# Values products of two attentions: split fp32r operands on the full array, or fp32 operands on two 64-column halves

## The chip, the cores and the metric

One core of a Trainium2 chip runs the whole kernel. The metric is device time in microseconds (us), the median of several executions. Beside it stands one profiled execution, whose trace gives the rows below.

## What is computed

Two layers of a hybrid decoder on x of 512 tokens by 1024 columns, all in float32. Each layer has a forgetting attention ("fox", 8 heads of 64) and a native sparse attention ("nsa", 8 heads of 64, two key/value heads; here a selected, a sliding-window and a compressed branch), then an MLP. What matters here is the last line of each attention, for one head and a block of 128 queries:

```python
p = softmax(q @ k.T * scale + bias, masked)     # 128 x 512 at most, causal
o = p @ v                                       # v: 512 x 64
# nsa: o_n = g0 * o_cmp + g1 * o_sel + g2 * o_win, then o_n @ w_o_nsa
```

## The kernel before

TensorE multiplies in two ways here. In fp32r, one pass over the moving columns, an operand is split into a high part and the remainder ("h", "lo"), and a product is made of two or three matmuls that accumulate in PSUM. In fp32, with operands unsplit, each matmul of the program becomes two recorded instructions (a weight load and a matmul each). Transposes on TensorE are fp32 with the identity.

`layer` (L781) first projects the values of all heads by token (`token_proj`). It splits them into `VF` (fox, L802 to L809) and `VN` (nsa, L811 to L824): 64 columns of high part and 64 columns of remainder side by side for each head, so that one 128-column weight load holds both. ScalarE (ACT) writes the high part, VectorE (DVE) the remainder. `forget` (L713) is a chain of small DVE steps that ends in a matmul (L738).

`attend` (L507) runs the units of an attention. A unit is one head of fox, or one head of one nsa branch; there are 8 units in fox and 16 in nsa in each layer, 48 in all. In step t it interleaves three generators and a filler: `scores` of unit t (two matmuls for each of four query blocks, then the DVE's masked minimum at L417 and ACT's exponential at L418, and at the end the scaling by the reciprocal sums, L449 and L451), `transposes` of unit t-1 (ten 128x128 transposes in three PSUM banks, L464; ACT writes the high part `pth`, L468, DVE the remainder `ptl`, L469), and `values` of unit t-2. In every round each generator advances once, and then the filler, which is the projections of the layer (`gemm`, L209, 512-column matmuls, six for a step), advances by `FOX_FILL` = 1.8 or `NSA_FILL` = 0.95 steps. The program's instructions get priorities in this order of issue; a scheduler then puts each engine's instructions in a fixed order when the kernel is built, an instruction being placed by priority among those that are ready.

`values` (L473) makes eight matmuls for a unit: key blocks 0 to 3 against 512, 384, 256 and 128 query columns, each with `pth` and `ptl`, stationary 128 columns (v high | v remainder). The two halves of the output bank O (partitions 0 to 63 and 64 to 127) have then to be added: `out_half` (L491) copies one half on ACT (L496) and adds on DVE (L497) into the pair's tile, once for each head; `out_pair` (L499) splits the finished pair of heads for the next projection. In nsa the two branches of a head accumulate in one bank, and `after` (L891) adds the compressed branch with one 512-column fp32r matmul on `self.vz` (L892).

`compress` (L538) already has a block of 64-column fp32 products (`product`, L573 to L584): two products with different operands go to partitions 0 to 63 and 64 to 127 of one bank, in turn; the first has its normal priority and the others are put 60 places ahead, so that they follow it at once. There are eight products in a block and four blocks in a layer (L575).

Of the kernel before, what the change touches and what calls it, by code (L numbers as in the profile page):

```python
# [11 lines left out]
F32 = mybir.dt.float32  # L12
F32R = mybir.dt.float32r
AF = mybir.ActivationFunctionType
OP = mybir.AluOpType
# [4 lines left out]
T = 512  # L20
KT = D // 128
NB = T // 128
# [120 lines left out]
class Body:  # L143
# [309 lines left out]
    def transposes(self, u):  # L453
        nc = self.nc
        E = u["E"]
        u["pt"] = []
        for g in range(3):
            ps = self.p("PT")
            if g < 2:
                todo = [(i, g) for i in range(g, NB)]  # L460
            else:
                todo = [(3, 3), (2, 2), (3, 2)]
            for j, (i, b) in enumerate(todo):
                nc.tensor.transpose(ps[:, j * 128:(j + 1) * 128], E[i][:, b * 128:(b + 1) * 128], self.ident)  # L464
            n = 128 * len(todo)
            h = self.t("t2", [128, T], F32R, name="pth")
            lo = self.t("t2", [128, T], F32R, name="ptl")
            nc.scalar.copy(h[:, :n], ps[:, :n])  # L468
            nc.vector.tensor_sub(lo[:, :n], ps[:, :n], h[:, :n].bitcast(F32))  # L469
            u["pt"].append((h, lo))  # L470
            yield

    def values(self, u):  # L473
        nc = self.nc
        if u.get("first", True):
            u["O"][0] = self.p("O")
        O = u["O"][0]
        first = u.get("first", True)
        pt = u["pt"]
        last = u.get("last", True)  # L480
        todo = [(0, 0, 0, 512), (1, 1, 0, 384), (2, 2, 128, 256), (3, 2, 0, 128)]
        for b, g, o, n in todo:
            v = u["v"](b)
            for f in range(2):
                nc.tensor.matmul(O[:, T - n:], v, pt[g][f][:, o:o + n],  # L485
                                 start=first and b == 0 and f == 0, stop=last and b == 3 and f == 1)
            yield
        if "after" in u:
            u["after"]()

    def out_half(self, O, o, e):  # L491

        nc = self.nc
        t = self.t("tmp", [128, T])
        s, f = slice(64 * e, 64 * e + 64), slice(64 * (1 - e), 64 * (1 - e) + 64)
        nc.scalar.copy(t[s], O[f])  # L496
        nc.vector.tensor_add(o[s], O[s], t[s])  # L497

    def out_pair(self, o):  # L499
        nc = self.nc  # L500
# [6 lines left out]
    def attend(self, units, fill, rate, lead):  # L507


        n = len(units)  # L510
        owed = 0.0
        for _ in range(lead):
            next(fill)
        for t in range(n + 2):
            gens = []
            if t < n:
                while not units[t]["ready"]():
                    next(fill)
                gens.append(self.scores(units[t]))
            if 1 <= t <= n:  # L520
                gens.append(self.transposes(units[t - 1]))
            if t >= 2:
                gens.append(self.values(units[t - 2]))
            while gens:
                for g in list(gens):
                    try:
                        next(g)
                    except StopIteration:
                        gens.remove(g)
                owed += rate  # L530
# [7 lines left out]
    def compress(self, kc, vc, small, l):  # L538

        nc, a = self.nc, self.a  # L540
        A = []
        for x, pos in ((kc, "pos_k"), (vc, "pos_v")):
            t = [self.t("t2", [128, 8, 2, 32], name="ca") for _ in range(2)]
            v = x.rearrange("p (n j r) -> p r j n", j=8, r=2)
            for half in range(2):
                nc.vector.memset(t[half][:, :, 1, 31], 0.0)
                o = OFF[pos] + 8 * half
# [39 lines left out]
        h = self.t("tmp", [128, 256])  # L587
        nc.scalar.copy(h, hp[:, :256])
        pt = self.p("S")
# [4 lines left out]
        g = self.t("tmp", [128, 4, 64], name="g")  # L594
# [25 lines left out]
        k = self.t("tmp", [128, 64])  # L620
# [8 lines left out]
        for e in range(2):  # L629
            s, c = slice(64 * e, 64 * e + 64), slice(64 + 32 * e, 96 + 32 * e)  # L630
            nc.scalar.copy(self.kcz[s, :, 0, c], k2[s])
            nc.gpsimd.tensor_sub(self.kcz[s, :, 1, c], k2[s], self.kcz[s, :, 0, c].bitcast(F32))
        v = self.t("tmp", [128, 2, 64])
# [2 lines left out]
            nc.vector.scalar_tensor_tensor(v[:, hk], pv[:, hk * 64:hk * 64 + 64], 0.5, b2v, op0=OP.mult, op1=OP.add)  # L636
        for k in range(4):
            s = slice(32 * k, 32 * k + 32)
            z = self.vz[s, :, k % 2]
            nc.scalar.copy(z[:, :, :64], v[s])  # L640
            nc.gpsimd.tensor_sub(z[:, :, 64:], v[s], z[:, :, :64].bitcast(F32))

    def cmp_probs(self, hk):

# [136 lines left out]
    def layer(self, l, u):  # L781
        nc, a = self.nc, self.a
# [18 lines left out]
                            self.CHUNKS[l])  # L801
        VF = []  # L802
        for b in range(NB):
            v = self.t("va", [128, 8, 128], F32R, name="vf")
            pv = va[b].rearrange("p (h d) -> p h d", h=8)
            nc.scalar.activation(v[:, :, :64], pv, AF.Copy, scale=rc[:, b:b + 1])
            nc.vector.scalar_tensor_tensor(v[:, :, 64:], pv, rc[:, b:b + 1], v[:, :, :64].bitcast(F32),
                                           op0=OP.mult, op1=OP.subtract)
            VF.append(v)  # L809
        run(g)  # L810
        VN = self.t("vn", [128, NB, 4, 128], F32R)  # L811
        z = self.t("z", [128, NB, 8])
        th = self.t("th", [128, NB, 24])
        rch = self.t("s4", [128, NB], name="rch")
        nc.vector.tensor_scalar(rch, rc, 0.5, None, op0=OP.mult)
        for b in range(NB):
            pv = g2[b][:, :256].rearrange("p (h d) -> p h d", h=4)
# [4 lines left out]
            nc.scalar.activation(VN[:, b, :, :64], pv, AF.Copy, scale=r)  # L822
            nc.vector.scalar_tensor_tensor(VN[:, b, :, 64:], pv, r, VN[:, b, :, :64].bitcast(F32),
                                           op0=OP.mult, op1=OP.subtract)  # L824
# [10 lines left out]
        st = {}  # L835
# [7 lines left out]
        def fox_unit(h):  # L843
            p, e = divmod(h, 2)
            un = dict(q=lambda: st["qa", p][0][:, e], qx=lambda: st["qa", p][1][e], k=lambda: st["ka", p][:, e], O=[None],
                      ready=lambda: ("qa", p) in st and ("ka", p) in st,
                      v=lambda b: VF[b][:, h])

            def after():
                if e == 0:  # L850
                    st["oa", p] = self.t("tmp2", [128, T], name="o")
                self.out_half(un["O"][0], st["oa", p], e)
                if e == 1:
                    st["oa", p] = self.out_pair(st["oa", p])
            un["after"] = after
            return un

# [28 lines left out]
        def nsa_units(h):  # L886
            p, e = divmod(h, 2)
            hk, r = divmod(h, 4)
            O = [None]

            def after():  # L891
                nc.tensor.matmul(O[0], self.vz[:, hk, r % 2], self.pc[hk][r // 2], start=False, stop=True)  # L892
                if e == 0:
                    st["ob", p] = self.t("tmp2", [128, T], name="o")
                self.out_half(O[0], st["ob", p], e)
                if e == 1:
                    st["ob", p] = self.out_pair(st["ob", p])
            q = lambda: st["qb", p][:, e]
            b_ = dict(ready=lambda: hk in self.pc, q=q, k=lambda: st["kw"][:, hk], O=O,
                      v=lambda b: VN[:, b, 2 + hk], first=False, last=False, gate=lambda: gt[:, :, 2, h], after=after)  # L900
            a_ = dict(ready=lambda: ("qb", p) in st and "kw" in st, q=q, k=lambda: st["ks"][:, hk], O=O,
                      v=lambda b: VN[:, b, hk], last=False, gate=lambda: gt[:, :, 1, h], mate=b_,
                      kk=lambda: self.kk[:, :, hk].rearrange("p f b t -> p f (b t)"))
            return [a_, b_]
# [32 lines left out]

        units = []
        for h in range(0, 8, 2):
            (a0, b0), (a1, b1) = nsa_units(h), nsa_units(h + 1)  # L940
# [180 lines left out]
class Pairs:  # L1121
# [275 lines left out]
    def product(self, ps, k, i, xs, new):  # L1397

        h, lo = self.ops[k][i]
        n = len(xs[i])  # L1400

        def mm(w, x, **kw):
            self.nc.tensor.matmul(ps, w, x, skip_group_check=True, **kw)  # L1403

        for p in range(n):
            c = slice(p * 128, (p + 1) * 128)
            xh, xl = xs[i][p]
            mm(h[:, c], xh, start=new and p == 0, stop=False)
            mm(h[:, c], xl, start=False, stop=False)
            mm(lo[:, c], xh, start=False, stop=p == n - 1)  # L1410
# [403 lines left out]
```

## Time and profile before

| | us |
|---|---|
| time before, median of 3 runs | 1467.99 (1467.97 to 1468.05) |
| profiled execution, first to last instruction | 1466.7 |
| difference, outside the profiled span | 1.3 |
| TensorE matmul (PE) busy | 1451.1, 99% |
| TensorE weight load (PEld) busy | 1262.2, 86% |
| DVE busy | 1207.9, 82% |
| ACT busy | 917.8, 63% |
| mean granted TensorE clock | 0.997 |

A matmul's recorded duration includes the way through the array, so the durations of neighbours overlap and a busy PE says little. What a matmul costs its engine is read from the start of one to the start of the next: a 512-column gemm matmul lasts 0.39 us and the next one starts 0.23 us later. Layer 0's fox attention lies at about 75 to 190 us of the span, its nsa attention up to 350 us; in layer 1 both lie about 724 us later.

### The profile page before, as it was taken

To read this page: it belongs to the slowest core of one execution; us is meant where nothing else is said; L and a number is where in the kernel's file an instruction comes from. 1 tells how busy PE (TensorE), PEld (TensorE's weight loads), DVE (VectorE), ACT (ScalarE), POOL (GpSimd) and SP (SyncE) were. 2 spreads that over 40 slices of the span, in tenths; PEclk is the share of its full clock that TensorE was granted. 3 is DMA by queue.
4 is the path that set the end of the run, shared out by engine and by line. 5 is a ranking of instruction groups with operands and counts; after the bars stand their busy time and mean duration, and the time that the engine had idled before them with its cause. 6 is when DMAs were issued, how large, how long until landed. Compare 5 with 4: busy or idle time off the path is not lost.

```text
span 1466.7 us, 23475 instructions
## 1 busy us (share of the span) xinstructions
PE 1451.1 (99%) x8312; PEld 1262.2 (86%) x8312; DVE 1207.9 (82%) x2498; ACT 917.8 (63%) x1888; POOL 136.6 (9%) x192
## 2 busy tenths in 40 slices
PE   9999999999999999999999999999999999999996
PEld 8877888888898999989887788888888989899995
DVE  6587988777789898989866779887787888989897
ACT  6375666664577575848454656666546766757575
POOL 2000100000011111111300001000000111111110
PEclk9999999999999999999999999999999999999998
DMA  7564522126447677677846644221353475767774
GB/s 254 168 156 136 151 87 67 64 73 201 136 116 181 172 178 185 173 169 215 251 133 166 185 110 123 86 73 58 111 165 98 131 172 160 178 166 182 184 187 108
DMA packets 79478, 216.72 MB, mean 148 GB/s; under 512 B 10113, under 2 KB 10497, under 8 KB 79361
## 3 DMA queue, kind: packets, MB, share of 16 engines
q1 hardware_dynamic: 59248, 164.34, 35.4%
q0 software_dynamic: 17664, 46.67, 17.4%
q10 hardware_dynamic: 2448, 4.22, 0.8%
q8 instruction: 65, 1.06, 0.3%
q14 instruction: 53, 0.43, 0.1%
HBM read 168.46 MB, written 6.29 MB: 119 GB/s over the span
## 4 chain that ended last, share of the span: by engine, by line
PE 94%; DVE 3%; ACT 2%; issue 1%; DMA 0%; POOL 0%; ACTq 0%; DVEq 0%
PE ps_mm L215 10%; PE ps_mm L216 10%; PE ps_mm L217 9%; PE ps_mm L1530 7%; PE ps_S L1530 7%; PE ps_mm L1403 6%; PE ps_PT L1403 6%; PE ps_S L1403 6%; PE ps_O L485 4%; PE ps_PT L464 4%; PE ps_O L1403 3%; PE ps_PT L1530 3%; PE ps_O L1530 3%; PE ps_S L429 2%; PE ps_S L432 2%; PE ps_O L575 1%
## 5 line engine op out<-in xcount | busy, mean ns | idle before, releaser
L215 PE MATMUL ps_mm<-uh,wh 128*128 128x512 f32 x480 | 191.3, 398 | 0.2
L216 PE MATMUL ps_mm<-ul,wh 128*128 128x512 f32 x480 | 189.2, 394 | 0.0
L217 PE MATMUL ps_mm<-uh,wl 128*128 128x512 f32 x480 | 188.4, 392 | 0.0
L189 ACT CAST wh<-raw 128x1024 fp32r<-128x1024 f32 (+2 forms) x111 | 112.6, 1014 | 88.9 <-PE ps_mm L216 46.2
L1512 ACT CAST sh<-raw 128x512 fp32r<-128x512 f32 x160 | 96.7, 620 | 78.2 <-DVE raw L1611 26.7
L190 DVE TENSOR_TENSOR wl<-raw,wh 128x1024 fp32r<-128x1024 f32 (+2 forms) x111 | 130.6, 1177 | 17.8 <-ACT wh L189 17.5
L418 ACT ACTIVATE E<-E,mx 128x512 f32<-128x512 f32 (+3 forms) x176 | 101.3, 576 | 49.0 <-DVE mx L417 48.1
L468 ACT CAST pth<-ps_PT 128x512 fp32r<-128x512 f32 x144 | 73.1, 514 | 76.1 <-PE ps_PT L464 75.5
L1520 DVE TENSOR_TENSOR sl<-raw,sh 128x512 fp32r<-128x512 f32 x160 | 106.6, 688 | 12.2 <-ACT sh L1512 12.0
L417 DVE CUSTOM_DVE_ANT_0 E<-ps_S,ct 128x512 f32<-128x512 f32 (+3 forms) x176 | 87.4, 502 | 30.6 <-PE ps_S L432 29.8
L469 DVE TENSOR_TENSOR ptl<-ps_PT,pth 128x512 fp32r<-128x512 f32 x144 | 84.8, 598 | 33.4 <-ACT pth L468 31.7
L217 PEld LDWEIGHTS ps_mm<-uh,wl 128*128 128x128 f32 x480 | 90.2, 188 | 18.5
L215 PEld LDWEIGHTS ps_mm<-uh,wh 128*128 128x128 f32 x480 | 90.3, 188 | 15.7 <-DVE tmp L337 0.8
L216 PEld LDWEIGHTS ps_mm<-ul,wh 128*128 128x128 f32 x480 | 90.4, 188 | 13.6
L1377 POOL DMA_DIRECT2D raw<-raw x32 | 27.9, 873 | 735.4 <-DVE sl L1370 194.6
L1356 ACT CAST sh<-raw 128x512 fp32r<-128x512 f32 x128 | 74.5, 618 | 34.2 <-DMA raw<-raw 27.0
L1370 DVE TENSOR_TENSOR sl<-raw,sh 128x512 fp32r<-128x512 f32 x128 | 84.0, 686 | 9.8 <-ACT sh L1356 9.6
L1403 PE MATMUL ps_S<-t,sh 128*128 128x256 f32 x384 | 83.0, 282 | 0.0
L464 PE MATMUL ps_PT<-ct,E 128*128 128x128 f32 x464 | 76.3, 275 | 0.9 <-ACT E L451 0.6
L1356 ACT CAST sh<-sx 128x512 fp32r<-128x512 f32 x96 | 58.4, 614 | 28.0 <-DVE sx L1338 24.4
L1403 PE MATMUL ps_S<-t,sl 128*128 128x256 f32 x256 | 72.0, 281 | 0.0
L1370 DVE TENSOR_TENSOR sl<-sx,sh 128x512 fp32r<-128x512 f32 x96 | 64.6, 687 | 7.7 <-ACT sh L1356 7.7
(446 smaller groups left out, 4402.9 us busy)
## 6 DMA issues: line engine op xcount, KB each, us to landing
raw<-wb SPq DMA_DIRECT2D x64, 512.0 KB
raw<-wup SPq DMA_DIRECT2D x64, 512.0 KB
raw<-wt POOLq DMA_DIRECT2D x48, 512.0 KB, 6.8
raw<-wt SPq DMA_DIRECT2D x32, 512.0 KB
sx<-wt SPq DMA_DIRECT2D x64, 256.0 KB
kd<-hl SPq DMA_DIRECT2D x40, 256.0 KB
w<-w SPq DMA_DIRECT2D x32, 256.0 KB
raw<-wo SPq DMA_DIRECT2D x16, 512.0 KB
```

Source lines behind the costliest of these rows:

```text
L189: nc.scalar.copy(h[:, :n], raw[:, :n])
L190: nc.vector.tensor_tensor(lo[:, :n], raw[:, :n], h[:, :n].bitcast(F32), op=OP.subtract)
L215: mm(ps, h[:, c], xh, start=start and i == 0, stop=False)
L216: mm(ps, h[:, c], xl, start=False, stop=False)
L217: mm(ps, lo[:, c], xh, start=False, stop=stop and i == ks - 1)
L418: nc.scalar.activation(e, e, AF.Exp, bias=mx, scale=-1.0, accum_out=sm[:, i:i + 1])
L464: nc.tensor.transpose(ps[:, j * 128:(j + 1) * 128], E[i][:, b * 128:(b + 1) * 128], self.ident)
L1356: self.nc.scalar.copy(h, self.source(k, i))
L1370: self.nc.vector.tensor_tensor(lo, self.source(k, i), h.bitcast(F32), op=OP.subtract)
L1403: self.nc.tensor.matmul(ps, w, x, skip_group_check=True, **kw)
L1520: self.nc.vector.tensor_tensor(lo, self.operand(d, i, p), h.bitcast(F32), op=OP.subtract)
L1530: self.nc.tensor.matmul(ps[t][:, cols], a[:, s], m, start=new and f == 0, stop=f == 2, skip_group_check=True)
```

## The change

The probabilities are no longer split: `transposes` writes one fp32 tile for each of the three banks, by ACT alone (L469 goes), and takes the banks in the order 2, 1, 0. `VF` and `VN` hold fp32 values of 64 columns a head, written by ACT alone (L807 and L823 go). `values` runs once for two units, in the steps t = 3, 5, 7, ...: after one empty turn it issues eight fp32 products of 64 columns, for head 0 into partitions 0 to 63 and for head 1 into 64 to 127 of one bank. `out_half` goes; `out_pair` reads the bank. In nsa both heads of a pair share a bank, and the compressed branch is added for both at once with two matmuls (high parts, then remainders). The diff, without the lines that only follow from this:

```diff
     def transposes(self, u):
-        u["pt"] = []
-        for g in range(3):
+        u["pt"] = {}
+        for g in (2, 1, 0):
...
-            h = self.t("t2", [128, T], F32R, name="pth")
-            lo = self.t("t2", [128, T], F32R, name="ptl")
-            nc.scalar.copy(h[:, :n], ps[:, :n])
-            nc.vector.tensor_sub(lo[:, :n], ps[:, :n], h[:, :n].bitcast(F32))
-            u["pt"].append((h, lo))
+            pt = u["pt"][g] = self.t("t2", [128, T], name="pt")
+            nc.scalar.copy(pt[:, :n], ps[:, :n])
             yield
-    def values(self, u):
+    def values(self, pair):
         nc = self.nc
+        u = pair[1]
         if u.get("first", True):
             u["O"][0] = self.p("O")
         O = u["O"][0]
-        todo = [(0, 0, 0, 512), (1, 1, 0, 384), (2, 2, 128, 256), (3, 2, 0, 128)]
-        for b, g, o, n in todo:
-            v = u["v"](b)
-            for f in range(2):
-                nc.tensor.matmul(O[:, T - n:], v, pt[g][f][:, o:o + n],
-                                 start=first and b == 0 and f == 0, stop=last and b == 3 and f == 1)
-            yield
+        first, last = u.get("first", True), u.get("last", True)
+        yield
+
+        def product(e, b):
+            g, o, n = ((0, 0, 512), (1, 0, 384), (2, 128, 256), (2, 0, 128))[b]
+            nc.tensor.matmul(O[64 * e:64 * e + 64, T - n:], pair[e]["v"](b), pair[e]["pt"][g][:, o:o + n],
+                             start=first and b == 0, stop=last and b == 3, skip_group_check=True)
+
+        product(1, 0)
+        with self.tc.high_priority(60):
+            product(0, 0)
+            for b in range(1, NB):
+                for e in range(2):
+                    product(e, b)
         if "after" in u:
             u["after"]()
-    def out_half(self, O, o, e):
...
     def attend(self, units, fill, rate, lead):
-            if t >= 2:
-                gens.append(self.values(units[t - 2]))
+            if t >= 3 and t % 2:
+                gens.append(self.values(units[t - 3:t - 1]))
...
-            v = self.t("va", [128, 8, 128], F32R, name="vf")
-            pv = va[b].rearrange("p (h d) -> p h d", h=8)
-            nc.scalar.activation(v[:, :, :64], pv, AF.Copy, scale=rc[:, b:b + 1])
-            nc.vector.scalar_tensor_tensor(v[:, :, 64:], pv, rc[:, b:b + 1], v[:, :, :64].bitcast(F32),
-                                           op0=OP.mult, op1=OP.subtract)
+            v = self.t("va", [128, 8, 64], name="vf")
+            nc.scalar.activation(v.rearrange("p h d -> p (h d)"), va[b], AF.Copy, scale=rc[:, b:b + 1])
...
             def after():
-                nc.tensor.matmul(O[0], self.vz[:, hk, r % 2], self.pc[hk][r // 2], start=False, stop=True)
-                if e == 0:
-                    st["ob", p] = self.t("tmp2", [128, T], name="o")
-                self.out_half(O[0], st["ob", p], e)
-                if e == 1:
-                    st["ob", p] = self.out_pair(st["ob", p])
+                for f in range(2):
+                    nc.tensor.matmul(O[0], self.vz[:, f, hk], self.pc[hk][r // 2], start=False, stop=f == 1,
+                                     skip_group_check=True)
+                st["ob", p] = self.out_pair(O[0])
```

## Rows read from the trace of the kernel before

**Rows 1.** The page: busy time of each engine, and the last chain's shares.

```profile
PE 1451.1 (99%) x8312; PEld 1262.2 (86%) x8312; DVE 1207.9 (82%) x2498; ACT 917.8 (63%) x1888; POOL 136.6 (9%) x192
...
PE 94%; DVE 3%; ACT 2%; issue 1%; DMA 0%; POOL 0%; ACTq 0%; DVEq 0%
```

**Rows 2.** Windows of layer 0's fox and nsa: length, PE, PEld, DVE, ACT, POOL busy.

```profile
75.00:200.00 125.00, 124.16 (x672) 99.95 (x671) 106.05 (x270) 81.27 (x187) 10.38 (x20) 1.00 0.51 136
200.00:360.00 160.00, 160.00 (x828) 135.41 (x827) 124.32 (x288) 96.89 (x211) 1.81 (x2) 1.00 0.32 103
```

**Rows 3.** Timeline of PE, values products in nsa: start, length, instruction.

```profile
258.56 0.47 PE L485 MATMUL ps_O<-pth,vn 128*128 128x512 f32 x1
258.88 0.39 PE L485 MATMUL ps_O<-ptl,vn 128*128 128x512 f32 x1
259.11 0.40 PE L215 MATMUL ps_mm<-uh,wh 128*128 128x512 f32 x1
...
263.60 0.28 PE L485 MATMUL ps_O<-ptl,vn 128*128 128x256 f32 x1
263.72 0.39 PE L215 MATMUL ps_mm<-uh,wh 128*128 128x512 f32 x1
...
265.58 0.23 PE L485 MATMUL ps_O<-pth,vn 128*128 128x128 f32 x1
265.64 0.27 PE L485 MATMUL ps_O<-ptl,vn 128*128 128x128 f32 x1
265.75 0.44 PE L215 MATMUL ps_mm<-uh,wh 128*128 128x512 f32 x1
```

**Rows 4.** Timeline of PE around two of compress's blocks (L575) in fox.

```profile
94.41 0.34 PE L485 MATMUL ps_O<-ptl,vf 128*128 128x384 f32 x1
94.68 1.95 PE L575 MATMUL ps_O<-w,ca 128*64 128x256 f32 x16
96.56 0.98 PE L464 MATMUL ps_PT<-ct,E 128*128 128x128 f32 x7
...
117.67 0.39 PE L429 MATMUL ps_S<-kd,q 128*128 128x256 f32 x1
117.89 0.28 PE L432 MATMUL ps_S<-kd,qx 128*128 128x256 f32 x1
```

**Rows 5.** Line L575: durations (min/median/max), and windows with instructions under way (x).

```profile
L575 PE MATMUL ps_O<-w,ca x128: 379/379/431, 94.7 to 852.7; 128*64 128x256 f32 x128
...
94.70:94.72 0.02, 0.02 (x2) 0.02 (x2) 1.00 0.99 205
94.90:94.92 0.02, 0.02 (x2) 0.00 (x0) 1.00 1.06 205
94.97:94.99 0.02, 0.02 (x4) 0.02 (x2) 1.00 0.95 205
```

**Rows 6.** Groups of DVE, 75 to 200 us: busy us, mean ns, idle before.

```profile
L469 DVE TENSOR_TENSOR ptl<-ps_PT,pth 128x384 fp32r<-128x384 f32 (+1 forms) x31 | 18.2, 602 | 7.9 <-ACT pth L468 7.7
...
L497 DVE TENSOR_TENSOR o<-ps_O,tmp 64x512 f32<-64x512 f32 x8 | 5.5, 682 | 0.7 <-ACT tmp L496 0.6
```

**Rows 7.** Waits of the weight load, whole span: us, times, longest.

```profile
PEld ps_PT L464 <- ACT E L451: 3.5, 8, 0.7
PEld ps_S L429 <- DVE mx L417: 2.8, 9, 0.7
...
PEld ps_O L485 <- DVE ptl L469: 1.1, 4, 0.4
```

**Rows 8.** Timeline of PE at the end of `forget`, layer 0.

```profile
51.47 0.39 PE L216 MATMUL ps_PT<-ul,wh 128*128 128x512 f32 x1
...
52.20 0.46 PE L738 MATMUL ps_S<-ones,fb 128*128 128x128 f32 x2 [0.34 <-DVE fb L736]
```

**Rows 9.** Timeline of PE before a unit's transposes in fox.

```profile
81.41 0.39 PE L217 MATMUL ps_mm<-uh,wl 128*128 128x512 f32 x1
82.09 0.66 PE L464 MATMUL ps_PT<-ct,E 128*128 128x128 f32 x4 [0.29 <-ACT E L451]
```

More of the change, by code (lines that the diff above doesn't have):

```diff
@@ L477, in values @@
         O = u["O"][0]
-        first = u.get("first", True)
-        pt = u["pt"]
-        last = u.get("last", True)
-        todo = [(0, 0, 0, 512), (1, 1, 0, 384), (2, 2, 128, 256), (3, 2, 0, 128)]
-        for b, g, o, n in todo:
-            v = u["v"](b)
-            for f in range(2):
-                nc.tensor.matmul(O[:, T - n:], v, pt[g][f][:, o:o + n],
-                                 start=first and b == 0 and f == 0, stop=last and b == 3 and f == 1)
-            yield
+        first, last = u.get("first", True), u.get("last", True)
[10 more added lines that the diff above has]
+                    product(e, b)
         if "after" in u:
             u["after"]()
-    def out_half(self, O, o, e):
[L493 to L497, printed above, removed]
     def out_pair(self, o):
@@ L638, in compress @@
             s = slice(32 * k, 32 * k + 32)
-            z = self.vz[s, :, k % 2]
-            nc.scalar.copy(z[:, :, :64], v[s])
-            nc.gpsimd.tensor_sub(z[:, :, 64:], v[s], z[:, :, :64].bitcast(F32))
+            c = slice(k % 2 * 64, k % 2 * 64 + 64)
+            nc.scalar.copy(self.vz[s, 0, :, c], v[s])
+            nc.gpsimd.tensor_sub(self.vz[s, 1, :, c], v[s], self.vz[s, 0, :, c].bitcast(F32))
     def cmp_probs(self, hk):
@@ L803, in layer @@
         for b in range(NB):
-            v = self.t("va", [128, 8, 128], F32R, name="vf")
-            pv = va[b].rearrange("p (h d) -> p h d", h=8)
-            nc.scalar.activation(v[:, :, :64], pv, AF.Copy, scale=rc[:, b:b + 1])
-            nc.vector.scalar_tensor_tensor(v[:, :, 64:], pv, rc[:, b:b + 1], v[:, :, :64].bitcast(F32),
-                                           op0=OP.mult, op1=OP.subtract)
+            v = self.t("va", [128, 8, 64], name="vf")
+            nc.scalar.activation(v.rearrange("p h d -> p (h d)"), va[b], AF.Copy, scale=rc[:, b:b + 1])
             VF.append(v)
         run(g)
-        VN = self.t("vn", [128, NB, 4, 128], F32R)
+        VN = self.t("vn", [128, NB, 4, 64])
         z = self.t("z", [128, NB, 8])
@@ L821, in layer @@
             nc.scalar.activation(th[:, b], g2[b][:, 264:288], AF.Tanh, scale=rch[:, b:b + 1])
-            nc.scalar.activation(VN[:, b, :, :64], pv, AF.Copy, scale=r)
-            nc.vector.scalar_tensor_tensor(VN[:, b, :, 64:], pv, r, VN[:, b, :, :64].bitcast(F32),
-                                           op0=OP.mult, op1=OP.subtract)
+            nc.scalar.activation(VN[:, b].rearrange("p h d -> p (h d)"), g2[b][:, :256], AF.Copy, scale=r)
         self.gates = gt = self.t("gates", [128, NB, 3, 8])
@@ L849, in after @@
             def after():
-                if e == 0:
-                    st["oa", p] = self.t("tmp2", [128, T], name="o")
-                self.out_half(un["O"][0], st["oa", p], e)
-                if e == 1:
-                    st["oa", p] = self.out_pair(st["oa", p])
+                st["oa", p] = self.out_pair(un["O"][0])
             un["after"] = after
@@ L884, in layer, with nsa_units @@
         ya = [st["oa", p] for p in range(4)]
-        def nsa_units(h):
+        def nsa_units(h, O):
             p, e = divmod(h, 2)
             hk, r = divmod(h, 4)
-            O = [None]
             def after():
-                nc.tensor.matmul(O[0], self.vz[:, hk, r % 2], self.pc[hk][r // 2], start=False, stop=True)
-                if e == 0:
-                    st["ob", p] = self.t("tmp2", [128, T], name="o")
-                self.out_half(O[0], st["ob", p], e)
-                if e == 1:
-                    st["ob", p] = self.out_pair(st["ob", p])
+                for f in range(2):
+                    nc.tensor.matmul(O[0], self.vz[:, f, hk], self.pc[hk][r // 2], start=False, stop=f == 1,
+                                     skip_group_check=True)
+                st["ob", p] = self.out_pair(O[0])
             q = lambda: st["qb", p][:, e]
@@ L939, in layer @@
         for h in range(0, 8, 2):
-            (a0, b0), (a1, b1) = nsa_units(h), nsa_units(h + 1)
+            O = [None]
+            (a0, b0), (a1, b1) = nsa_units(h, O), nsa_units(h + 1, O)
             units += [a0, a1, b0, b1]
```

1 line of the change is left out of this document (removed).

## The prediction

> **What bounds the kernel now.** I read the page first: TensorE has a matmul under way in 1451.1 of 1466.7 us and 94% of the last chain is PE [rows 1]. Busy counts a matmul's way through the array, so I then took the windows of the two attentions: in nsa PE has no idle time at all in 160 us, in fox 0.84 us in 125, while DVE is busy for 106 us (85%) and ACT for 81 in fox, 124 and 97 in nsa [rows 2]. So an attention lasts as long as its matmuls take from start to start, and DVE and ACT matter only where a weight load waits for them. The list of waits says how much that is: 3.5 us for ACT's scaled exponentials (L451), 2.8 for the DVE's minima (L417), 1.1 for `ptl`, in the whole span [rows 7]. The change takes work from DVE, which is not the bound, and rebuilds 384 of PE's matmuls, which are. The answer has to come from PE's starts.
>
> **Value products before, on PE.** In nsa a remainder product of 512 columns starts at 258.88 and hands over at 259.11: 0.23 us. The high product before it seems to take 0.32, but the last transpose ahead of it gave way correspondingly early, so I count 0.23 for it too. 256 columns take 0.12, and the two of 128 columns 0.17 together (265.58 to 265.75) [rows 3]. 384 columns, by columns between 512 and 256: 0.175 (estimate). A unit: 2 x (0.23 + 0.175 + 0.12) + 0.17 = 1.22 us; a pair of heads 2.44; 24 pairs in both layers 58.6 us.
>
> **Value products after, on PE.** The trace has the same kind of work: compress's blocks, eight fp32 products of 64 columns that alternate between the halves, recorded as 16 matmuls of 256 columns [rows 4]. Two run at once from the start: two are under way at 94.70 and at 94.90, four at 94.97, when the next two have begun and the ends of the first two still show [rows 5]. The block ends at 94.68 + 1.95 = 96.63; its last two matmuls last 0.379 and so start at 96.25; the second two start near 94.95 [rows 4, 5]. That is 1.30 us over six rounds, 0.217 us a round, in which each half does one recorded matmul of 256 columns. Eight rounds are 1.74 us. The whole block, from where the 384-column matmul before it would have handed over (94.41 + 0.175) to the next start at 96.56, takes 1.97 [rows 4]: 0.24 is fixed, for going in and out. The next matmul can pay too: the score matmul at 117.67 takes 0.22 to its successor [rows 4], where 256 columns take 0.12 [rows 3]: 0.10 more.
> The new block has two recorded matmuls for each product, and on each half 512 + 384 + 256 + 128 = 1280 columns, twice: 2560 columns, or ten rounds: 2.17 us. With 0.24 fixed that is 2.41, with the neighbour's 0.10 it is 2.51. I take 2.48, since most neighbours will be gemm or score matmuls: 24 x 2.48 = 59.5 us, against 58.6 **+0.9 us** (bounds 24 x 2.41 = 57.8 and 24 x 2.51 = 60.2, -0.8 to +1.6). So the array streams the same columns: before, the second half of its columns worked on the remainder's share of the same head; now that half has a head of its own, and fp32 takes twice the passes. Nothing is won there, and the fixed price eats what little there is. The compressed branch has two matmuls a pair before and after, the transposes and scores stay as they are: zero.
>
> **DVE, ACT and POOL.** DVE loses 144 `ptl` (31 of them, 18.2 us, in this window) and 32 additions (8, 5.5 us) [rows 6]: 106 - 23.7 = 82 us of 125 in fox. ACT loses the 32 half copies and keeps its 144 evictions. The split of the values also goes from DVE, eight steps in each layer just before `forget`. `out_pair` now reads the bank in place of a tile; half of what it does is what L469 did, at the same size: zero. POOL's remainders for `vz` keep their number. No DMA is added, removed or moved past another one. All of this lies beside PE; it is worth only the waits that it shortens.
> First, `forget`: PE's order is fixed, and L738 holds back PE until DVE has done L736: from 51.47 to 52.20, 0.73 where 0.23 is normal [rows 8]. With eight DVE steps less ahead of it I take this wait as gone: 0.5 us a layer, **-1.0 us** (bounds 0 and -1.0).
> Second, the attention's waits: those listed sum to 7.4 us of weight-load idle time [rows 7]. Not all of that is lost on PE: at 81.41 the next start comes after 0.68 where 0.23 is normal, 0.45 lost [rows 9], where the longest idle time of the load is 0.7 [rows 7]. The wait for `ptl` must go, as there is no `ptl`; those for DVE's minima should shrink with 22% less DVE work in fox; those for ACT shrink less, since ACT keeps its evictions. Bounds 0 and -7.4; I take about half: **-3.5 us**.
>
> **What is moved.** A pair's products come in one piece, 2.5 us in which no score or transpose starts. The chains of scores behind them wait that long on PE; DVE and ACT have the slack for it, by the windows. The block reads first what is written last (bank 0 of the second head, now the last of the three); between that eviction and the block lie about three rounds with their filler, some three filler steps of six 0.23 us matmuls in nsa, about 4 us, against an eviction of about 0.6 us like `ptl`'s [rows 6]: covered; without the cover each block would wait up to 0.6, 14 us in all. Since `values` turns only twice, nsa's steps have fewer rounds: I count 78 in place of 90, so 76 of the filler's 88 steps are used inside, where it was 87.5. Twelve steps (16 us of gemm) come after the last unit. They are needed anyway and hide the last `out_pair`: zero.
>
> **Sum.** 0.9 - 1.0 - 3.5 = -3.6 us: 1466.7 - 3.6 = 1463.1 for the profiled span. The median of the runs is 1.3 us above that span, which stays: **1464.4 us**.
>
> **Rivals.** (a) The waits only change owner. For it: the wait at 81.41 is for ACT, not DVE [rows 9], and blocks of 2.5 us make the work around them more uneven. Against: DVE feeds ACT's exponentials. Only the block's price would be left, 1468.0 + 0.9 = 1468.9, no change.
> (b) The array takes matmuls strictly in program order. Products come as head 1, 0, 0, 1, 0, 1, 0, 1, each as two recorded matmuls on one half. In strict order, half 1 would stand idle from the end of its two 512-column matmuls until the second 512-column and the first 384-column one of half 0 had run: 0.43 + 0.33 = 0.76 us a block by the round above, 24 x 0.76 = 18 us: 1482.6, slower. It decides from the second product of the block on. Against it: in strict order one matmul alone would be under way at 94.70 and 94.90, as the second one of a product needs the half of the first; the trace has two [rows 5]. The Trainium skill, "TensorE: Matmul & The Clock Gate", Part 3, "What overlaps and what doesn't", says that matmuls start and end in strict program order. By that rule the time would be this rival's; the trace does not agree with it for two halves.
> (c) 64-column matmuls of 512 moving columns do not run side by side; the trace shows it for 256 only. Each block would take ten rounds more: 24 x 2.17 = 52 us, 1517, slower.
> (d) All the waits go, and the block's price is at its low end: -0.8 - 1.0 - 7.4 = -9.2; more likely two thirds of it, about 1461.
>
> **How the numbers follow.** A measurement of this kernel can tell about 0.2%, 2.9 us, from no change. Forecast 57%, 1462 to 1467, three quarters of it below 1465.05; (a) 26%, 1467 to 1470.5; (d) 8%, 1459.5 to 1462; (b) 6%; (c) 3%. Faster: 43 + 8 = 51%. Slower: 6 + 3 and one of (a): 10%. Same: 39%. The range 1459.5 to 1470.5 takes in the forecast, (a) and (d), some 90%, less what their own ends may miss; (b) and (c) are left out.
>
> **What would show it.** The blocks: 24 rows of 16 64-column matmuls on the new line of `product`, each 2.3 to 2.6 us to the next start, with pairs that begin together; 3.2 us would be (b), 4.6 (c). DVE near 82 us in fox's window. L738 without idle time before it. The list of the load's waits: without `ptl`, the sum for L451 and L417 under 4 us; if it stays at 6 or a wait for L449 (the third group's first transpose now needs the last scaled row first) takes its place, (a) holds. The prediction is wrong if blocks stand apart from their second product, if a block waits for its own evictions, or if gemm matmuls lengthen beside it.

## The result and the profile after

| | before | after |
|---|---|---|
| time, median | 1468.02 (1467.97 to 1468.13) | 1478.76 (1478.38 to 1479.46) |
| profiled execution, first to last instruction | 1466.7 | 1477.6 |

The changed kernel is slower: 1.0073 of the time before, 95% interval 1.0061 to 1.0084, 10.7 us. The forecast was 1464.4, and the range ended at 1470.5.

In the changed kernel the products stand in line 481, `forget`'s matmul in line 732 (738 before), `ptl` is gone, and the one copy of a bank is line 467. First the page (busy time, shares of the last chain), then the windows of layer 0's fox and nsa with the columns of [rows 2]:

```profile
PE 1454.1 (98%) x8312; PEld 1230.3 (83%) x8312; DVE 1103.2 (75%) x2306; ACT 893.7 (60%) x1856; POOL 137.5 (9%) x192
...
PE 92%; DVE 5%; ACT 1%; issue 1%; DMA 1%; POOL 0%; SPq 0%; DVEq 0%; ACTq 0%
```

```profile
75.00:200.00 125.00, 120.71 (x644) 91.56 (x642) 81.29 (x227) 74.43 (x175) 11.69 (x22) 0.99 0.52 141
200.00:360.00 160.00, 159.61 (x828) 123.88 (x827) 95.01 (x238) 89.33 (x204) 1.82 (x2) 1.00 0.30 93
```

DVE does what was forecast: 81.3 us in fox, where 82 was worked out and 106 stood before [rows 2]. PE does not: it now has 4.3 us without a matmul under way in fox, where it had 0.84, and DVE's share of the chain rises from 3% to 5% although DVE does 105 us less [rows 1].

The list of waits for PE's own matmuls (us in total, times, longest), after and then before. It counts what PE itself stood still by the records; from start to start a wait costs up to 0.16 us more, since a 512-column matmul is recorded for 0.39 us and hands over after 0.23. The list of [rows 7] counts the weight load, which runs ahead of the matmuls:

```profile
PE ps_S L429 <- DVE qs L354: 4.7, 2, 2.4
PE ps_S L429 <- DVE mx L417: 2.1, 2, 1.0
...
PE ps_PT L464 <- DVE E L449: 1.1, 2, 0.5
PE ps_mm L215 <- DVE tmp L337: 0.6, 2, 0.3
...
PE ps_S L732 <- DVE fb L730: 0.5, 2, 0.2
```

```profile
PE ps_S L738 <- DVE fb L736: 0.7, 2, 0.3
PE ps_PT L464 <- ACT E L451: 0.6, 2, 0.3
PE ps_S L429 <- DVE mx L417: 0.6, 2, 0.3
```

Those of the layers sum to 9.0 us after and 1.9 before: 7.1 of the 10.9 us by which the span grew. Each comes twice, once a layer. At the start of the kernel PE stands still another 0.8 us more (L323, 1.0 for 0.2); over all the profiles of this case that wait lies between nothing and 1.0 us. The timeline of PE in the changed kernel shows a block that is cut, an ordinary one, and the largest wait:

```profile
91.69 0.40 PE L217 MATMUL ps_mm<-uh,wl 128*128 128x512 f32 x1
92.02 1.08 PE L481 MATMUL ps_O<-pt,vf 128*64 128x512 f32 x4
93.03 0.50 PE L429 MATMUL ps_S<-kd,q 128*128 128x512 f32 x1
93.45 0.86 PE L481 MATMUL ps_O<-pt,vf 128*64 128x384 f32 x2
94.24 0.50 PE L432 MATMUL ps_S<-kd,qx 128*128 128x512 f32 x1
94.67 1.51 PE L481 MATMUL ps_O<-pt,vf 128*64 128x384 f32 x10
96.11 0.39 PE L429 MATMUL ps_S<-kd,q 128*128 128x256 f32 x1
...
120.86 2.38 PE L481 MATMUL ps_O<-pt,vf 128*64 128x512 f32 x16
123.17 0.50 PE L215 MATMUL ps_mm<-uh,wh 128*128 128x512 f32 x1
123.50 0.39 PE L216 MATMUL ps_mm<-ul,wh 128*128 128x512 f32 x1
...
159.93 0.39 PE L429 MATMUL ps_S<-kd,q 128*128 128x512 f32 x1
...
163.57 0.39 PE L217 MATMUL ps_mm<-uh,wl 128*128 128x512 f32 x1
166.38 0.36 PE L429 MATMUL ps_S<-kk,q 128*128 128x256 f32 x1 [2.42 <-DVE qs L354]
```

- **An ordinary block** (22 of 24) is 16 matmuls in one piece, 2.31 us from its first start to the next one (120.86 to 123.17), and the matmul behind it takes 0.33 to its successor, 0.10 more than 0.23. With 0.09 ahead of its first start it costs 2.40 and 0.10 on the neighbour: the price that was forecast, 2.41 and 0.10.
- **The first block of each layer** is cut in three by two scores: three times into the 64-column form and out again. From start to start, less what a neighbour of its shape takes, the pieces cost 1.11 + 0.99 + 1.64 = 3.73 us (rounded) in place of 2.40. That is 2.7 us for both layers. Two things make up the 1.33 of a block (an estimate from the rows): going in and out twice more costs 2 x (0.24 + 0.10) = 0.68, and the middle piece has one 384-column product alone, so the two products of 384 columns run one after the other, two rounds more of 0.32, 0.65.
- **The hand-over from fox to nsa.** The first score of nsa (on `kk`) holds PE from 163.80, when it was free, to 166.38. It needs two copies of nsa's first keys (`kk`), made by DMAs that POOL issues when DVE has split the keys, and two of the first queries (`q`), whose DMAs SP issues. The list puts the wait down to DVE's L354. But in both layers, here and in e2 below, the score starts 0.35 us after the second copy of the keys has landed (at 166.03 here): it waits for the keys. POOL's timeline and the time from issue to landing of the four copies of keys, after and then before:

```profile
160.59 2.56 POOL L365 DMA_DIRECT2D kk<-hl  x4 [2.06 <-DVE hl L354]
...
DMA to landing us min/median/max: 3.9/4.3/4.7
```

```profile
157.35 2.56 POOL L365 DMA_DIRECT2D kk<-hl  x4 [2.54 <-DVE hl L354]
...
DMA to landing us min/median/max: 2.6/2.9/3.2
```

And PE's timeline before:

```profile
157.28 0.39 PE L429 MATMUL ps_S<-kd,q 128*128 128x512 f32 x1
...
157.74 0.23 PE L485 MATMUL ps_O<-pth,vf 128*128 128x128 f32 x1
...
160.30 0.44 PE L216 MATMUL ps_mm<-ul,wh 128*128 128x512 f32 x1
160.58 0.39 PE L217 MATMUL ps_mm<-uh,wl 128*128 128x512 f32 x1
...
163.00 0.28 PE L429 MATMUL ps_S<-kk,q 128*128 128x256 f32 x1
...
165.33 0.50 PE L485 MATMUL ps_O<-pth,vf 128*128 128x512 f32 x1
```

Before, the second copy landed at 161.01. With the 0.35 that leaves some 1.6 us to spare at 163.00 (1.3 in layer 1). What is to spare stands in no list of waits. Counted from the last score of fox (157.28 before, 159.93 after), three things used it up and more. PE comes to nsa's first score 1.85 us sooner, after 3.87 in place of 5.72: the products of unit 6 and the last two of unit 5 lay in between, 1.55 us (157.74 to 158.90 and 159.91 to 160.30), and are now in blocks elsewhere, those of unit 6 at 172.51. (Unit 7's stood behind the score before, too, from 165.33.) The keys are issued 0.59 us later: in DVE's order a split of weights (L190, 1.22 us) and the remainder of the queries now stand ahead of their split. And their second copy takes 4.66 us to land in place of 2.88, 1.78 more. Together these are 4.2 us, and 4.2 less 1.6 is the 2.6 that PE waits. As to the slower copies: the mean busy share of the DMA engines was 0.94 while they ran, and 0.70 before, and SP had issued 512 KB of weights (`wo`) at 157.70, ahead of them, where before it came at 159.96, behind them. No run tests this alone.

After these 2.4 us of idle time the clock falls. Windows of PE after, with the columns of [rows 2]; the granted clock is the third number from the end:

```profile
168.00:169.00 1.00, 1.00 (x4) 0.80 (x3) 0.00 (x0) 0.00 (x0) 0.00 (x0) 0.50 1.04 295
...
172.00:174.00 2.00, 2.00 (x11) 0.77 (x12) 0.43 (x2) 1.63 (x6) 0.00 (x0) 1.00 0.37 92
```

It is at 0.50 (1.2 GHz) from about 167.8 to 171.2, when PE has long been busy again: some 1.7 us. In layer 1 the same wait is not followed by it.

**The account:** waits in the layers 7.1, cut blocks 2.7, the clock 1.7, together 11.5. On the other side the array itself became cheaper. A unit before costs 0.05 more than my 1.22, since the matmul behind its last two products takes 0.28 to its successor (160.30 to 160.58). That makes 48 x 1.27 = 61.0 us, against 24 x 2.50 = 60.0 for ordinary blocks: -1.0. The sum is +10.5 of 10.9 us; with the 0.8 at the kernel's start it is 11.3, so it is good to half a us or so.

### The profile page after: what moved, and what is told of

Read it like the earlier page. It is cut to its first block, busy times and chain, and to the rows that moved or that the text cites. A ratio compares the mean times of both kernels' runs of the same rounds, so it can differ in the third digit from the quotient of the medians.

```text
span 1477.6 us, 23251 instructions
## 1 busy us (share of the span) xinstructions
PE 1454.1 (98%) x8312; PEld 1230.3 (83%) x8312; DVE 1103.2 (75%) x2306; ACT 893.7 (60%) x1856; POOL 137.5 (9%) x192
## 4 chain that ended last, share of the span: by engine, by line
PE 92%; DVE 5%; ACT 1%; issue 1%; DMA 1%; POOL 0%; SPq 0%; DVEq 0%; ACTq 0%
PE ps_mm L215 9%; PE ps_mm L217 9%; PE ps_mm L216 9%; PE ps_mm L1512 7%; PE ps_S L1512 7%; PE ps_mm L1385 6%; PE ps_PT L1385 6%; PE ps_S L1385 6%; PE ps_PT L464 4%; PE ps_O L481 4%; PE ps_O L1385 3%; PE ps_O L1512 3%; PE ps_PT L1512 3%; PE ps_S L429 2%; PE ps_S L432 2%; DVE wl L190 1%
## 5 line engine op out<-in xcount | busy, mean ns | idle before, releaser
L215 PE MATMUL ps_mm<-uh,wh 128*128 128x512 f32 x480 | 195.2, 407 | 0.6 <-DVE tmp L337 0.6
L417 DVE CUSTOM_DVE_ANT_0 E<-ps_S,ct 128x512 f32<-128x512 f32 (+3 forms) x176 | 87.6, 503 | 87.0 <-PE ps_S L432 86.9
L190 DVE TENSOR_TENSOR wl<-raw,wh 128x1024 fp32r<-128x1024 f32 (+2 forms) x111 | 130.8, 1178 | 27.0 <-ACT wh L189 26.7
L467 ACT COPY pt<-ps_PT 128x384 f32<-128x384 f32 x144 | 72.1, 512 | 81.8 <-PE ps_PT L464 80.8
L464 PE MATMUL ps_PT<-ct,E 128*128 128x128 f32 x464 | 73.4, 278 | 1.9 <-DVE E L449 1.1
L464 PEld LDWEIGHTS ps_PT<-ct,E 128*128 128x128 f32 x464 | 55.0, 142 | 19.0 <-issue 8.1
```

The costliest lines, as they stand in the source:

```text
L190: nc.vector.tensor_tensor(lo[:, :n], raw[:, :n], h[:, :n].bitcast(F32), op=OP.subtract)
L215: mm(ps, h[:, c], xh, start=start and i == 0, stop=False)
```

## Experiments

Theory 1 is that account: the array does what was forecast, and the loss is lost cover (work of PE that hides what another engine or a DMA does) in PE's fixed order. Theory 2 is that the blocks themselves cost more than the starts show. The kernel before, run beside them, took 1468.80 (e1 to e4), 1468.23 (e5 to e8) and 1468.25 us (e9 to e12). Times are medians, with the ratio's 95% interval.

**e1.** Two more filler steps (2 x 6 x 0.23 = 2.8 us) ahead of nsa's first scores.

```diff
-        self.attend(units, fill2(), self.NSA_FILL, 2)
+        self.attend(units, fill2(), self.NSA_FILL, 4)
```

> The changed kernel with two more filler steps (twelve gemm matmuls) ahead of nsa's first scores: lead 4 in place of 2. In the trace of the changed kernel those scores hold PE for 2.4 us at 163.8 and 2.2 us at 894. Theory 1 (the change lost the cover at this hand-over, and the wait is a fixed date, not work): PE's idle time there goes and the time falls by 4 to 5 us, to about 1474. Theory 2 (the loss lies in the blocks' own price on the array): the wait moves but the time stays within 1 us of 1478.8.

1472.68 us, 1.0027 (1.0017 to 1.0037): 6.1 less than the changed kernel. The wait for `qs` has left the list, and no clock of 0.5 follows; its price, 4.7 + 1.7 = 6.4 us, is what came back. The block of units 6 and 7 (168.17) now stands ahead of nsa's first score (171.20), six us after the keys have landed (165.17). The other waits stay as they were, and the first block of each layer is still cut in three.

**e2.** The rest of a block is put 100 places ahead.

```diff
-        with self.tc.high_priority(60):
+        with self.tc.high_priority(100):
```

> The changed kernel with the block's products put 100 places ahead in place of 60. In fox's first block of each layer two scores then no longer stand between its products; all else of the fixed order ahead of the attention's end stays. Read from the trace, the split block costs 3.7 us against 2.4: theory 1 expects 2 to 3 us less, about 1476.3. Theory 3 (what a split costs, the waits after it give back): within 0.7 us of 1478.8.

1475.22 us, 1.0044 (1.0029 to 1.0059): 3.5 less, more than the 2 to 3 expected. The first block is in one piece, the hand-over waits less too (3.3 for 4.7), and in the profiled execution the clock does not fall behind it. Its timeline and its waits:

```profile
91.69 2.38 PE L481 MATMUL ps_O<-pt,vf 128*64 128x512 f32 x16
94.00 0.50 PE L429 MATMUL ps_S<-kd,q 128*128 128x512 f32 x1
```

```profile
PE ps_S L429 <- DVE E L449: 1.7, 1, 1.7
PE ps_S L429 <- DMA kk<-hl: 1.6, 1, 1.6
```

Here the wait is put down to the DMA of `kk` in one layer and to DVE's L449 in the other. The name is whatever ended last by the records; in both layers the score starts 0.35 us after the keys' second copy.

**e3.** The kernel before without the remainder of the probabilities.

```diff
-            lo = self.t("t2", [128, T], F32R, name="ptl")
...
-            nc.vector.tensor_sub(lo[:, :n], ps[:, :n], h[:, :n].bitcast(F32))
-            u["pt"].append((h, lo))
+            u["pt"].append((h, h))
```

> The kernel before, without the 144 remainders of the probabilities on DVE; the remainder's products stay and read the high part again, so that the output is not the reference's. It takes the change's relief of DVE alone. The forecast's step (half of the waits go): 3.5 us less than before, 1464.5. Rival (the waits change owner): within 1 us of 1468.

1469.68 us, 1.0008 (0.9999 to 1.0017). DVE has 16 us less to do in fox (90.3 in place of 106.1) and nothing is won: the forecast's gain does not come. PE's wait for the minima (0.6 before) grew, and one for ACT is new:

```profile
PE ps_S L429 <- DVE mx L417: 1.0, 2, 0.5
PE ps_S L649 <- ACT qs L353: 0.9, 2, 0.4
```

**e4.** The kernel before with its own split products, but those of two units issued together at t = 3, 5, 7.

```diff
-            if t >= 2:
-                gens.append(self.values(units[t - 2]))
+            if t >= 3 and t % 2:
+                gens.append(self.pair(units[t - 3:t - 1]))
...
+    def pair(self, units):
+        yield
+        for u in units:
+            run(self.values(u))
```

> The kernel before, with the values products of two units issued together in one piece after one empty turn, in the steps t = 3, 5, 7, ..., as in the change; operands, array and DVE's work stay those of before. It takes the move alone. Theory 1 (the move takes cover from the waits): 3 to 8 us more than before, 1471 to 1476, with idle time at the first scores of nsa. Theory 2 (the move is free, the array's halves cost the time): within 1 us of 1468.

1479.68 us, 1.0078 (1.0062 to 1.0095), more than expected. With the probabilities' products all in fp32r on the full array, the move alone costs as much as the whole change. Its largest wait is at the same score and of the same size, but for the other operand. The wait, and SP's issue of the queries' copies, here and in the kernel before:

```profile
PE ps_S L429 <- DMA q<-qs: 4.7, 2, 2.4
...
160.49 10.14 SPq L388 DMA_DIRECT2D q<-qs  x8
```

```profile
157.13 2.78 SPq L388 DMA_DIRECT2D q<-qs  x4
```

The keys' copies landed in 2.1 us here, the second at 161.29. The second copy of the queries was issued at 161.50 (157.64 before), took 4.9 us in place of 3.1 and landed at 166.40, 0.13 ahead of the score. Unit 6's products did not leave their place: they still stand ahead of the score (158.62 to 161.32), and PE has about 5.5 us of work behind the keys' issue, as before. So at the hand-over the move does not cost by lost products alone: in the new orders of the other engines an operand of that score comes late, here the queries, in the changed kernel the keys. Of the 9.5 us by which this profiled span is longer than that of the kernel before, 6.5 are idle time of PE; the other 3 stay open.

**e5.** Both repairs, e1's and e2's, in the changed kernel.

> The changed kernel with both repairs of the order at once: four filler steps ahead of nsa's first scores in place of two, and the rest of a block put 100 places ahead in place of 60. Theory 1 (the loss is lost cover in PE's fixed order, the block's own price is as forecast): the two add, less the part of the hand-over wait that the second repair already took (2.5 to 1.7 us a layer): 1478.8 - 6.1 - 3.5 + 1.6 = 1470.8, within 1469.5 to 1472, with a first block of 16 in one piece and no wait for qs, kk or q on L429. Theory 2 (the fp32 blocks cost more than the split products in a way that no start-to-start shows): the two do not add, and it stays at 1472.5 or above.

1469.69 us, 1.0010 (1.0000 to 1.0019). They add as theory 1 has it, within its band. No wait at the hand-over is left.

**e6.** e5 with the banks in the order 0, 1, 2.

```diff
-        for g in (2, 1, 0):
+        for g in (0, 1, 2):
```

> As e5, and the transposes take the banks in the order 0, 1, 2 again, as in the kernel before. The wait of a unit's first transposes for the last scaled row (L464 for L449, 0.5 us each on PE at 152.9 and 877, and two or three of 0.1 in nsa) then falls away, as the group that needs it comes last. Theory 1: 0.6 to 1.5 us less than e5, 1469.5 or so. Rival: the block then waits for the eviction that comes last (bank 2 is read by its third product only), or the wait goes to ACT's L451 as in the kernel before: no gain over e5, or up to 1 us more.

1466.82 us, 0.9991 (0.9982 to 1.0000): 2.9 less than e5, more than expected. The wait of L464 for L449 is gone (1.1) and the one for L417 shrank from 2.0 to 1.7; the rest of the 2.9 stays open. No block waits for its evictions.

**e7.** The kernel before with e1's edit.

> The kernel before with four filler steps ahead of nsa's first scores in place of two. Theory 1 (the two steps pay only where the values products have left the hand-over uncovered): the kernel before has no wait there, so 1467.5 to 1469, no change. Rival (the lead was too short in the kernel before as well, and the gain of e1 has nothing to do with the change): 2 us or more below the kernel before.

1481.81 us, 1.0091 (1.0076 to 1.0107). This was a miss, and the most useful one. The edit that brings the changed kernel 6.1 us costs the kernel before 13.6. PE's timeline at the end of nsa, here and in the kernel before:

```profile
349.80 0.39 PE L892 MATMUL ps_O<-cp,vz 128*128 128x512 f32 x1
...
351.84 0.39 PE L217 MATMUL ps_mm<-oh,wl 128*128 128x512 f32 x1
354.92 0.77 PE L215 MATMUL ps_mm<-oh,wh 128*128 128x512 f32 x1 [2.69 <-ACT oh L503]
```

```profile
345.30 0.39 PE L892 MATMUL ps_O<-cp,vz 128*128 128x512 f32 x1
...
348.25 0.39 PE L215 MATMUL ps_mm<-oh,wh 128*128 128x512 f32 x1
```

ACT's copy of the last `out_pair`, here and before:

```profile
354.25 0.61 ACT L503 CAST oh<-o 128x512 fp32r<-128x512 f32 x1
```

```profile
347.61 0.62 ACT L503 CAST oh<-o 128x512 fp32r<-128x512 f32 x1 [0.88 <-DVE o L497]
```

Before, twelve gemm matmuls of the filler (345.53 to 348.25, 2.7 us) and nine of the output projection, on the three pairs that are ready, lie between the last product and the first use of the last pair: 5.0 us (345.30 to 350.29). `oh` was ready after 2.9 (348.23). Two filler steps are twelve matmuls: spent at the front they are missing here, and 2.3 us are left (349.80 to 352.07). And `oh` now takes 5.1 us (to 354.86), as a split of weights on DVE (L190) and casts of weights on ACT (L1356) have come to stand in the midst of its steps. The projection waits 2.7 and 2.6 us in the two layers, and each time the clock is then at 0.50 for more than 3 us: 1.7 us more a layer. That is 8.7 of the 13.6; the rest stays open.

**e8.** e4 with e1's edit.

> The kernel before with the products of two units issued together (as e4) and four filler steps ahead of nsa's first scores. Theory 1: the 2.4 us a layer that L429 waited for q in e4 go, as in the changed kernel: 1479.7 - 5 = 1474.7, within 1473.5 to 1476.5. Rival (in e4 the loss lay elsewhere, in DVE's remainders that stand between the transposes and the block): under 2 us less than e4, 1477.7 or more.

1473.64 us, 1.0038 (1.0023 to 1.0053): 6.0 less than e4. At the hand-over the paired order with the split products is mended by the same two steps, and no wait for `oh` comes at the end of nsa; 5.4 us stay lost.

**e9.** e6 once more, with more runs.

> The kernel of e6 once more, beside more runs of the kernel before: whether the changed kernel with its order mended is ahead of the kernel before. Theory 1: 0.9985 to 0.9995 of it, 1.0 to 2.2 us less. Rival (e6's lead was the spread of the runs): 1.0000 or above.

1466.83 us, 0.9991 (0.9982 to 1.0000), the same as e6. The changed kernel with its order mended is 1.4 us ahead of the kernel before, at the edge of what these runs can tell. Its waits in the layers sum to 3.0 us (1.7 for L417, 0.7 for L337, 0.6 for L730), 1.1 more than before. With the array's -1.0 that should leave it level; its span is 1464.8, 1.9 us shorter than before, and what these 2 us are stays open. So the two ways of multiplying are about level, and what was lost lay in the order.

**e10.** e6 with the products of one head after those of the other.

```diff
-            product(0, 0)
             for b in range(1, NB):
-                for e in range(2):
-                    product(e, b)
+                product(1, b)
+            for b in range(NB):
+                product(0, b)
```

> The kernel of e6 with a block's products in another order: all four of head 1, then all four of head 0, in place of in turn. The arithmetic is the same. If a half of the array takes its matmuls from a queue of its own, however far down the program they stand: no change, 1466.8. If the halves run at once only where the products of both stand next to each other in the program: a block takes 20 rounds of 0.217 us in place of ten, 2.17 us more, 24 of them 52 us: 1519. Between the two (1470 to 1510) if only some instructions are looked at ahead.

1503.46 us, 1.0241 (1.0227 to 1.0255): between the two. 22 of the 24 blocks take 3.86 us from their first start to the next one, where it was 2.31. The timeline has a block of 3.93 us, and the windows show how many matmuls are under way (x, PE first):

```profile
91.61 3.93 PE L481 MATMUL ps_O<-pt,vf 128*64 128x512 f32 x16
```

```profile
92.40:92.42 0.02, 0.02 (x1) 0.00 (x0) 0.02 (x1) 0.02 (x2) 0.00 (x0) 1.00 0.99 410
...
94.60:94.62 0.02, 0.02 (x1) 0.00 (x0) 0.00 (x0) 0.00 (x0) 0.00 (x0) 1.00 4.37 819
```

At 92.40 and 94.60 one matmul runs alone, where in turn two do, as in [rows 5]. By the recorded starts of the 16, the first matmul of head 0 (the ninth, if PE's order is the kernel's order of issue) starts at +1.560 us, 6 ns behind the fifth of head 1 (+1.554), and so ahead of the sixth to eighth, which start at +1.770, +1.986 and +2.095. So one half overtook three matmuls of the other and no more. The halves work side by side only from there to about +2.2, and a block costs 3.96 us in place of 2.40: 24 x 1.56 = 37 us, and e10 is 36.6 us behind e9.

**e11.** e6 with 15 filler steps ahead of nsa's first scores in place of 4.

> The kernel of e6 with 15 filler steps ahead of nsa's first scores in place of 4, which is all that stands behind the last unit there (22 gemm triples, eleven steps, at 332 to 346.3 us). Theory 1 (filler behind the last unit is a reserve: it costs nothing to spend until none is left to hide the last out_pair): the output projection waits for oh as in e7, 2.7 us and about 0.9 behind it in each layer, 1466.8 + 7 = 1474, within 1471 to 1478. Rival (the loss of e7 lay in the later start of nsa's scores): more is lost here, in proportion to eleven steps against two, 1490 or above; or nothing, if the last out_pair is hidden by the projection itself.

1472.45 us, 1.0027 (1.0016 to 1.0038), 5.6 more than e6 and inside theory 1's band. But its mechanism is only in part what is seen: what waits is not `oh` but the remainder behind it (L498), 0.8, and more is lost on the gates that the last filler steps had to make ready:

```profile
PE ps_mm L215 <- DVE gate L943: 1.5, 2, 0.9
...
PE ps_mm L216 <- DVE ol L498: 0.8, 2, 0.4
```

**e12.** e6 with another fill.

```diff
-    FOX_FILL = 1.8
+    FOX_FILL = 2.0
```

> The kernel of e6 with FOX_FILL 2.0 in place of 1.8: more gemm in each round of fox. At 88.7 us L429 waits 0.8 us a layer for the minima of its bank, which stand behind a remainder of weights (L190, 1.2 us, itself waiting for ACT) in DVE's order. Theory 1 (these waits follow from which step of DVE stands ahead of which, and so from the fill): that wait changes, and others with it, within 1.5 us either way of 1466.8. Rival (only the length of the cover matters): the wait falls and 1 to 2 us are won, 1465.3.

1473.34 us, 1.0035 (1.0022 to 1.0049): 6.5 more than e6, outside both expectations. More gemm in a round of fox did not lengthen the cover where it was wanted; three waits grew or came, 4.2 us more together, 2.4 for L417 (1.7 in e6) and these (0.7 and nothing in e6):

```profile
PE ps_mm L215 <- DVE tmp L337: 2.4, 2, 1.2
PE ps_PT L464 <- ACT E L451: 1.8, 2, 0.9
```

## Why the prediction was wrong

**The price of a block was right.** 2.41 us and 0.10 on the neighbour were forecast from `compress`'s blocks, and 2.40 and 0.10 measured. Rivals (b) and (c) are false: two matmuls run at once also at 512 columns. The Trainium skill, "TensorE: Matmul & The Clock Gate", Part 3, "What overlaps and what doesn't", has matmuls start in strict program order. The trace does not agree for matmuls on two halves: in a block, matmuls that are not neighbours in the program start 6 to 8 ns apart, and in e10 one starts ahead of three earlier ones. That e10 loses 37 us shows how short the reach of this is, and that the order in turn is what the price rests on.

**The term of the products before was a little low**: 58.6 for 61.0, as the price on the neighbour was counted for the blocks only. So the +0.9 of the sum was -1.0. Alone it would have made the forecast too high.

**The -3.5 of the DVE's relief was wrong, and could have been seen to be.** What it halved was idle time of the weight load [rows 7], which runs ahead. What PE itself stood still is in the list of PE's waits, 0.6 + 0.6 us in the attentions of both layers, and the windows say the same: 0.84 us of 125 in fox, none in nsa [rows 2]. With the 0.16 that each of these four waits may hide, that is 1.8 us, and waits too short to show can add to it; half of 7.4 was not there to be had. e3 takes 16 us of DVE work out of fox and wins nothing (1469.7 against 1468.8): one wait grew and one came. That such waits hang on which step stands ahead in an engine's order, more than on how full the engine is, fits e3 and e12, but no run tests it alone. Rival (a), the waits change owner, was right about this term.

**The -1.0 of `forget` was a miss too.** L732 still waits 0.25 us in each layer, as against 0.33 before. So eight steps less on DVE took 0.2 us in all from this wait; what holds the rest stays open.

**"What is moved: zero" is the step that failed.** It had the facts: the pair's products come in one piece and later, and twelve filler steps come behind the last unit (13 in the trace). It asked what hides the moved work, and found enough. It did not ask what the moved work had hidden, nor what a new order does to the dates of operands that other engines and DMAs make. Measured from the last score of fox, PE now comes 1.85 us sooner to nsa's first score, 1.55 of that products that had stood in between, and the keys land 2.4 us later, where 1.6 us were to spare: a wait of 2.4 us a layer, with the clock 6.4 us in all. A stretch that is covered stands in no list of waits, however little is to spare, so my look at the waits could not find it. e4 shows that the move alone, with the arithmetic of before, costs 10.9 us, 4.7 of them as a wait at the same score, there for the queries; e1, e5 and e8 give the hand-over's part back with two filler steps. Which new order makes which copy late is read from the traces and not tested by itself. The filler for it lay as 13 steps behind the last unit, where two could be spared without a wait (e1) and all of them could not (e11).

**The cut blocks** were named as what would make the prediction wrong ("blocks stand apart from their second product"), but with no price or chance. At 1.3 us a layer and 60 places ahead that was a rival worth working out.

**No rival was slower by this mechanism.** The one that should have stood there: the new order leaves the first score of nsa waiting for its DMAs, some 2.5 us in each layer, and a clock that can fall behind such a gap.

## What to carry to other kernels

When work is moved in a fixed order, list what started behind it and was waited for in its old place (DMAs issued, evictions, chains on other engines), and measure from landing to first use what is to spare: a stretch that is covered shows no wait, however little that is. A new order can make the same copy land later, too: from issue to landing 2.9 us in one order and 4.3 in the other. Bound what relief of a helper engine can bring by the time that the bound engine itself loses, from start to start, not by the idle time of its weight load. Filler is a stock: before judging a new order of the work, look where it now lies and where it is missing. The same two steps were worth 6.1 us in one kernel and cost 13.6 in the other.

## What the runs showed of the hardware

- Matmuls on the two column halves do not keep program order between them: one starts ahead of three earlier ones of the other half (e10), and in these runs not of more. In turn, two heads take 2.40 us; one after the other 3.96.
- Going from the full array to the 64-column halves and back cost 0.24 us a block, and 0.10 more on the matmul behind. In three pieces, the same 16 matmuls cost 3.73 us in place of 2.40, about half of the difference for going in and out twice more and half for two products that no longer ran side by side.
- The same four 64 KB copies took 2.1 us (median) from issue to landing at a mean busy share of the DMA engines of 0.46 (e4), 2.9 at 0.70 (before) and 4.3 at 0.94 (after).
- After 2.4 to 2.7 us without a matmul the granted clock fell to 0.50 in three of the places seen (the hand-over of layer 0 after, both ends of nsa in e7): 1.4 us after the matmuls had resumed in the first, 0.1 and 0.6 us after in e7, and for 3.4 us each time. In three places with gaps of 2.2 to 2.4 us (layer 1 after, both layers of e4) it stayed at 1.00. What tells them apart stays open.
